# Linear attention's decay levels: prefix sums and exponentials replaced by running products of block decays, on 64x64 quarters of the array

## The chip, the cores and the metric

The kernel runs on one core of one Trainium2 chip. The metric is the device time of one execution in microseconds; lower is better. Three runs of the kernel before took 316.83, 316.96 and 317.05 us (median 316.96 us).

## The reference, cut to what matters

One decoder layer on 256 tokens of width 1024. One input projection of the normalised x feeds two kinds of heads side by side: eight softmax heads of 64 (here each query simply attends causally, since 256 tokens are one block) and four heads of gated linear attention with key width 64 and value width 128. Their outputs are joined, projected and added to x; a gated feed-forward part with a short causal convolution and a last normalisation follow.

The linear attention is the part that changes. With a decay alpha per token and key channel:

```
S_t = diag(alpha_t) S_{t-1} + k_t^T v_t ;  o_t = q_t S_t
A[t,s] = sum_d q[t,d] k[s,d] prod_{s < u <= t} alpha[u,d]     (s <= t)
o = A v
```

So every pair (t, s) needs the product of the decays between s and t, per channel.

## The kernel before, in words

**The whole.** Matmuls against weights are done in three passes (`mm3`, L108): each operand is split into a rounded high part and the rest, and high x high, high x low and low x high are added. ScalarE makes the high parts of the weights (L92), VectorE the low parts (L95). Small attention matmuls are plain fp32, which the array takes as two passes each. TensorE's instructions stand in the order in which the program writes them (`manual_schedule` for PE); the order on VectorE and ScalarE is laid out by the framework's scheduler from dependencies and priority, with the softmax steps raised (`tc.high_priority`).

**The order around the change.** Steps q = 0 to 47 run the input projection: six groups of eight steps (gate inputs, softmax q, softmax k, softmax v, linear v, linear gate r), each step one slice of 128 of the contraction, twelve `mm3` passes of 256 columns or six of 512. Steps 48 to 63 are the output projection, and after them comes the feed-forward part. A table `plan`, filled by `on(q, f, ...)` (L537), names what is written ahead of the matmuls of step q: at equal q, in the order in which it was entered. The attention work thus lies between projection matmuls.

**Linear attention.** The gate is a log-sigmoid (`g_gate`, L301); `g_scan` (L314) makes its running sum `Gc` within each 128 tokens. The 128x128 score blocks are made by levels b = 32, 16, 8, 4, 2, 1, 64: at level b, a query in the second half of a 2b-token block meets the keys in its first half, with the block's middle as pivot. `lvl_a` (L321) subtracts on VectorE (L330, L331) and exponentiates on ScalarE (L332); `lvl_b` (L335) multiplies keys (L345) and, for each of the two heads of a pair, queries (L351) into zero-padded buffers `kts` and `qts`; `lvl_c` (L353) does eight matmuls on 128x64 halves of the array (L363; level 64: four with 128 columns on one half, L358); `lvl_d_` (L368) copies the level's entries out of PSUM by a mask (L377). `l128_a` to `l128_c` (L383 to L405) do the same between the two 128-token halves. `g_av` (L413) multiplies by v at step 46. The levels' matmuls stand at steps 25, 27, 30, 33, 36, 38 and 41, those of `l128_c` at 44.

**Softmax heads.** `m_scores` (L480) makes the scores of two heads on 64x128 halves of the array (L487), at steps 30, 33, 36 and 39; `m_softmax1` and `m_softmax2` (L490, L504), `m_pt` (transposes, L515) and `m_av` (L527, L528; steps 38, 41, 44 and 47) follow.

**PSUM.** Four banks (`acc`) serve the projections; four (`att`) are handed out in turn to everything else: each level, each score tile, each transpose and each `m_av` takes the next one and waits until its last reader is done.

Of the kernel before, what the change touches and what calls it, by code (L numbers as in the profile page):

```python
# [22 lines left out]
TAU = 16.0  # L23
# [1 line left out]
NP = DFF // 128  # L25
EPS = 1e-6
NG = 256 + RANK + 256
LEVELS = [32, 16, 8, 4, 2, 1, 64]

P_FG, P_BG, P_CW, P_CB = 0, 8, 10, 10 + 3 * 2 * NP  # L30
NPAR = P_CB + 2 * NP
# [3 lines left out]
def trunk_kernel(ctx: ExitStack, tc: tile.TileContext, xT_d, wG_d, w5_d, wo_d, up_d, dn_d,  # L35
                 par_d, gla_g_d, fin_g_d, wgu_d, cos_d, sin_d, causal_d, lvl_d, ident_d, out_d):
    nc = tc.nc
    V, A, T, DMA = nc.vector, nc.scalar, nc.tensor, nc.sync
# [11 lines left out]
    def att():  # L50
        return ps_att.tile([128, 512], F32, name="att")
# [7 lines left out]
    lvl = const.tile([128, len(LEVELS), 32], F32, name="lvl")  # L59
# [140 lines left out]
    at = ap_.enter_context(tc.tile_pool(name="attn", bufs=1))  # L200
    gqk = at.tile([128, 2, NG], F32, name="gqk")
    gqT = at.tile([128, 2, S], F32, name="gqT")
    gkT = at.tile([128, 2, S], F32, name="gkT")
    Gc = at.tile([128, 512], F32, name="Gc")
    ATd = at.tile([128, 8, 64], F32, name="ATd")
    AT = at.tile([128, 8, 128], F32, name="ATf")
    AT01 = at.tile([128, 4, 128], F32, name="AT01")
    lrT = at.tile([RANK, S], F32, name="lrT")
    kts = [at.tile([128, 512], F32, name=f"kt{i}") for i in range(2)]
    qts = [at.tile([128, 4, 2, 64], F32, name=f"qt{i}") for i in range(2)]  # L210
    qt128 = at.tile([128, 2, 2, 128], F32, name="qt128")
    resets = at.tile([128, 512], F32, name="y", bufs=2)
    nc.gpsimd.memset(resets, 1.0)
    nc.gpsimd.memset(resets.rearrange("p (n t) -> p n t", t=128)[:, :, 0:1], 0.0)
    for i in range(2):
        nc.gpsimd.memset(kts[i], 0.0)
        nc.gpsimd.memset(qts[i], 0.0)
    nc.gpsimd.memset(qt128, 0.0)
    nc.gpsimd.memset(AT[64:128, :, 0:64], 0.0)
    mqT = at.tile([128, 4, S], F32, name="mqT")  # L220
    mkT = at.tile([128, 4, S], F32, name="mkT")
# [9 lines left out]
    st = {}  # L231
# [41 lines left out]
    def g_transpose(which):  # L273
        p = att()
        o, dst, sc = ((0, gqT, DK ** -0.5), (272, gkT, 1.0))[which]
        for pr in range(2):
            for tt in range(2):
                c = pr * S + tt * 128
                T.transpose(p[:, c:c + 128], gqk[:, tt, o + pr * 128:o + (pr + 1) * 128], ident)
        A.activation(dst.rearrange("p a t -> p (a t)"), p, AF.Copy, scale=sc)  # L280

    def g_diag():
        dgp = at.tile([128, 2, 256], F32, name="e", bufs=2)
# [27 lines left out]
        A.activation(e, e, AF.Ln, bias=1.0)  # L311
        st["mn"], st["ln"] = mn, e

    def g_scan():  # L314
        la = at.tile([128, 512], F32, name="d", bufs=2)
        V.tensor_sub(la, st["mn"], st["ln"])
        V.tensor_tensor_scan(Gc, resets, la, 0.0, op0=ALU.mult, op1=ALU.add)

    lv = {}

    def lvl_a(l):  # L321
        b = LEVELS[l]
        d = at.tile([128, 512], F32, name="d", bufs=2)
        e = at.tile([128, 512], F32, name="e", bufs=2)
        dv = d.rearrange("p (n two b) -> p n two b", two=2, b=b)
        gvw = Gc.rearrange("p (n two b) -> p n two b", two=2, b=b)
        n = 256 // b
        piv = gvw[:, :, 0, b - 1:b]
        pb = piv.to_broadcast([128, n, b])
        V.tensor_sub(dv[:, :, 0, :], pb, gvw[:, :, 0, :])  # L330
        V.tensor_sub(dv[:, :, 1, :], gvw[:, :, 1, :], pb)  # L331
        A.activation(e, d, AF.Exp, scale=1.0 / TAU)  # L332
        lv[l] = e

    def lvl_b(l):  # L335
        b = LEVELS[l]
        e = lv[l]
        kt, qt = kts[l % 2], qts[l % 2]

        def blk(x):  # L340
            return x.rearrange("p (n two b) -> p n two b", two=2, b=b)

        gk_ = gkT.rearrange("p a t -> p (a t)")
        gq_ = gqT.rearrange("p a t -> p (a t)")
        V.tensor_mul(blk(kt)[:, :, 0, :], blk(gk_)[:, :, 0, :], blk(e)[:, :, 0, :])  # L345
        for h in range(2):
            ps = slice(64 * h, 64 * h + 64)
            o = qt[ps, :, h, :].rearrange("p g (n b) -> p g n b", b=b)
            q_ = gq_[ps].rearrange("p (g n two b) -> p g n two b", g=4, two=2, b=b)[:, :, :, 1, :]
            e_ = e[ps].rearrange("p (g n two b) -> p g n two b", g=4, two=2, b=b)[:, :, :, 1, :]  # L350
            V.tensor_mul(o, q_, e_)  # L351

    def lvl_c(l):  # L353
        kt, qt = kts[l % 2], qts[l % 2]
        p = att()
        if LEVELS[l] == 64:
            for g in range(4):
                T.matmul(p[0:64, g * 128:(g + 1) * 128], kt[:, g * 128:g * 128 + 64],  # L358
                         qt[:, g].rearrange("p h t -> p (h t)"), start=True, stop=True)
        else:  # L360
            for g in range(4):
                for j in range(2):
                    T.matmul(p[64 * j:64 * j + 64, g * 64:(g + 1) * 64],  # L363
                             kt[:, g * 128 + 64 * j:g * 128 + 64 * j + 64],
                             qt[:, g, :, 32 * j:32 * j + 32], start=True, stop=True)
        st["lv", l] = p

    def lvl_d_(l):  # L368
        b = LEVELS[l]
        p = st["lv", l]  # L370
        if b == 64:
            A.activation(AT[0:64, :, 64:128], p[0:64].rearrange("p (i t) -> p i t", i=8), AF.Copy)
            return
        n = 32 // b
        o = ATd.rearrange("p i (n two b) -> p i n two b", two=2, b=b)[:, :, :, 1, :]
        m = lvl[:, l].bitcast(I32).rearrange("p (n b) -> p n b", b=b)[:, None].to_broadcast([128, 8, n, b])
        V.copy_predicated(o, m, p[:, :256].rearrange("p (i n b) -> p i n b", i=8, b=b))  # L377
# [5 lines left out]
    def l128_a():  # L383
        d = at.tile([128, 2, 128], F32, name="d", bufs=2)
        e = at.tile([128, 2, 2, 128], F32, name="e", bufs=2)
        G4 = Gc.rearrange("p (a b t) -> p a b t", a=2, b=2)
        V.tensor_sub(d, G4[:, :, 0, 127:128].to_broadcast([128, 2, 128]), G4[:, :, 0, :])
        A.activation(e[:, 0], d, AF.Exp, scale=1.0 / TAU)
        A.activation(e[:, 1], G4[:, :, 1, :], AF.Exp, scale=1.0 / TAU)
        lv["128"] = e  # L390

    def l128_b():
        e = lv["128"]
        kt = kts[1].rearrange("p (a t) -> p a t", a=4)
        V.tensor_mul(kt[:, 0:2], gkT[:, :, 0:128], e[:, 0])
        for h in range(2):
            ps = slice(64 * h, 64 * h + 64)
            V.tensor_mul(qt128[ps, :, h, :], gqT[ps, :, 128:256], e[ps, 1])

    def l128_c():  # L400
        p = att()
        for pr in range(2):
            T.matmul(p[:, pr * 256:(pr + 1) * 256], kts[1][:, pr * 128:(pr + 1) * 128],
                     qt128[:, pr].rearrange("p h t -> p (h t)"), start=True, stop=True)
        A.activation(AT01.rearrange("p a t -> p (a t)"), p, AF.Copy)  # L405

    def gv_evac(tt):
        A.activation(gv[:, tt], st["gv"][tt], AF.Copy, scale=rstd(tt))
# [70 lines left out]

    def m_scores(pr):  # L480

        for hh in range(2):
            st["s", 2 * pr + hh] = att()
        for c0, c1 in ((0, 128), (128, 384)):
            for hh in range(2):
                ps = slice(64 * hh, 64 * hh + 64)
                T.matmul(st["s", 2 * pr + hh][:, c0:c1], mqT[ps, pr, c0:c0 + 128], mkT[ps, pr, 0:c1 - c0],  # L487
                         start=True, stop=True)

    def m_softmax1(h):  # L490
        with tc.high_priority():
# [45 lines left out]
    def on(q, f, *a):  # L537
        plan.setdefault(q, []).append((f, a))
# [21 lines left out]
    on(16, g_diag)  # L560
    on(12, g_gate_mm)
    on(12, g_gate)
    on(14, g_scan)
    for l in range(7):
        b = 21 + 11 * l // 4
        on(b, lvl_a, l)
        on(b + 1, lvl_b, l)
        on(b + 4, lvl_c, l)
        on(b + 5, lvl_d_, l)
    on(b + 5, lvl_join)  # L570
    on(39, l128_a)
    on(42, l128_b)
    on(44, l128_c)
    for tt in range(2):
        on(19 + 3 * tt, rope_b, 0, tt)
        on(27 + tt, rope_b, 1, tt)
        on(32, mv_evac, tt)
        on(40, gv_evac, tt)
    for h in range(HM):
        b = 30 + 3 * h // 2  # L580
        if h % 2 == 0:
            on(b, m_scores, h // 2)
        on(b + 1, m_softmax1, h)
        on(b + 2, m_softmax2, h)
        on(b + 4, m_pt, h)
        if h % 2:
            on(b + 7, m_av, h // 2)
    on(46, g_av, 0)
    on(46, g_av, 1)
    on(49, g_tail)  # L590
# [22 lines left out]
    for q in range(48):  # L613
        g, k = divmod(q, 8)
# [34 lines left out]
    for q in range(48, 64):  # L649
        ph, j = divmod(q - 48, 8)  # L650
# [264 lines left out]
    n = NP - 1  # L915
# [115 lines left out]
```

## Time and profile before

| what | value |
|---|---|
| median of three runs | 316.96 us |
| the profiled execution | 317.14 us, its span 315.4 us |
| granted TensorE clock, mean | 0.996 |
| TensorE busy | 306.6 us (97% of the span), 2296 matmul passes |
| VectorE busy | 252.9 us (80%), 472 instructions |
| ScalarE busy | 203.8 us (65%), 370 instructions |
| GpSimd busy | 3.9 us (1%) |

The span is the time from the first to the last instruction of the profiled execution; 1.7 us of its time lie around it. TensorE matmuls are pipelined, so their ends overlap: how fast the array goes is read from the distance between starts, not from busy time.

### The profile page before, as it was taken

The numbers are of one execution on the slowest core, as the hardware profiler recorded it, in microseconds if no ns is written. First come the engines' busy times: TensorE is split into PE (matmuls) and PEld (weight loads), VectorE is DVE, ScalarE is ACT, GpSimd is POOL, SyncE is SP. The second block draws the span as 40 slices with busy tenths as digits, with TensorE's granted clock in tenths as the row PEclk, the third lists the DMA queues.
The fourth block names the chain that finished last, engine by engine and source line by source line (L and its number), as shares of the span: only waits on it lengthen the run. The fifth ranks groups of instructions, "written<-read, shape, count | busy, mean of one in ns | idle before, by whom it ended". The sixth has DMA issues, their size and how long they took to land.

```text
span 315.4 us, 5840 instructions
## 1 busy us (share of the span) xinstructions
PE 306.6 (97%) x2296; PEld 283.1 (90%) x2296; DVE 252.9 (80%) x472; ACT 203.8 (65%) x370; POOL 3.9 (1%) x17
## 2 busy tenths in 40 slices
PE   7899999999999999999999999999999999999992
PEld 6899997776888999999999999999999999999982
DVE  3887999999647677999999988877777777776643
ACT  5878989497858478367676556666665555544362
POOL 4000000000000000000000000000000000000000
PEclk9999999999999999999999999999999999999998
DMA  7999533342361525496555664545555622120003
GB/s 199 374 413 411 201 135 133 133 150 120 135 219 50 178 90 200 157 380 268 200 202 200 225 220 177 195 185 202 201 202 200 262 72 69 67 69 0 2 0 135
DMA packets 12444, 55.40 MB, mean 176 GB/s; under 512 B 1392, under 2 KB 3200, under 8 KB 8064
## 3 DMA queue, kind: packets, MB, share of 16 engines
q1 hardware_dynamic: 12272, 54.76, 47.2%
q8 instruction: 18, 0.29, 0.3%
q10 hardware_dynamic: 144, 0.26, 0.2%
q14 instruction: 10, 0.08, 0.1%
HBM read 53.97 MB, written 1.05 MB: 174 GB/s over the span
## 4 chain that ended last, share of the span: by engine, by line
PE 79%; DVE 9%; ACT 5%; issue 2%; DMA 2%; SPq 1%; DVEq 0%; ACTq 0%
PE att L109 14%; PE att L111 14%; PE att L110 14%; PE acc L110 11%; PE acc L109 10%; PE acc L111 10%; DVE lo L95 2%; DMA xg<-in_xT 2%; ACT qs L466 1%; DVE qt L351 1%; DVE att L495 1%; ACT hi L92 1%; PE att L527 1%; DVE ATd L377 1%; DVE kt L345 1%
## 5 line engine op out<-in xcount | busy, mean ns | idle before, releaser
L92 ACT ACTIVATE hi<-raw 128x1024 fp32r<-128x1024 f32 (+3 forms) x84 | 80.1, 971 | 50.9 <-PE att L110 43.2
L95 DVE TENSOR_TENSOR lo<-raw,hi 128x1024 fp32r<-128x1024 f32 (+3 forms) x86 | 93.7, 1098 | 13.3 <-ACT hi L92 13.2
L109 PE MATMUL att<-hh,hi 128*128 128x256 f32 x352 | 98.5, 280 | 0.0
L111 PE MATMUL att<-hh,lo 128*128 128x256 f32 x352 | 98.4, 279 | 0.0
L110 PE MATMUL att<-hl,hi 128*128 128x256 f32 x352 | 98.3, 279 | 0.0
L109 PEld LDWEIGHTS att<-hh,hi 128*128 128x128 f32 x352 | 66.2, 188 | 0.0
L111 PEld LDWEIGHTS att<-hh,lo 128*128 128x128 f32 x352 | 66.2, 188 | 0.0
L110 PEld LDWEIGHTS att<-hl,hi 128*128 128x128 f32 x352 | 66.2, 188 | 0.0
L757 DVE SCALAR_TENSOR_TENSOR c<-us,par,c 128x256 f32<-128x256 f32 x88 | 40.7, 482 | 4.1 <-ACT c L749 2.5
L749 ACT ACTIVATE c<-us,par 128x256 f32<-128x256 f32 x44 | 24.0, 591 | 21.5 <-DVE us L739 16.0
L111 PE MATMUL acc<-dhi,gl 128*128 128x512 f32 (+1 forms) x88 | 32.3, 367 | 0.0
L110 PE MATMUL acc<-dlo,gh 128*128 128x512 f32 (+1 forms) x88 | 32.2, 366 | 0.0
L109 PE MATMUL acc<-dhi,gh 128*128 128x512 f32 (+1 forms) x88 | 31.8, 361 | 0.0
L696 DVE TENSOR_TENSOR dlo<-draw,dhi 128x1024 fp32r<-128x1024 f32 x22 | 26.6, 1218 | 0.0
L739 DVE TENSOR_TENSOR us<-att,rb 128x512 f32<-128x512 f32 x20 | 13.8, 688 | 15.9 <-PE att L111 15.9
L109 PE MATMUL acc<-hi,ah 128*128 128x512 f32 (+1 forms) x64 | 25.6, 399 | 0.7 <-ACT hi L92 0.7
L110 PE MATMUL acc<-lo,ah 128*128 128x512 f32 (+1 forms) x64 | 24.2, 378 | 0.7 <-DVE lo L95 0.7
L111 PE MATMUL acc<-hi,al 128*128 128x512 f32 (+1 forms) x64 | 23.7, 371 | 0.0
L691 ACT ACTIVATE dhi<-draw 128x1024 fp32r<-128x1024 f32 x22 | 23.1, 1050 | 0.0
L110 PEld LDWEIGHTS acc<-dlo,gh 128*128 128x128 f32 x88 | 16.5, 188 | 3.0
L109 PEld LDWEIGHTS acc<-dhi,gh 128*128 128x128 f32 x88 | 16.6, 188 | 2.9
L111 PEld LDWEIGHTS acc<-dhi,gl 128*128 128x128 f32 x88 | 16.5, 188 | 2.6
(191 smaller groups left out, 528.9 us busy)
## 6 DMA issues: line engine op xcount, KB each, us to landing
raw<-in_up SPq DMA_DIRECT2D x22, 1024.0 KB, 4.8
draw<-in_dn SPq DMA_DIRECT2D x22, 512.0 KB, 5.7
raw<-in_w SPq DMA_DIRECT2D x8, 1024.0 KB, 7.3
raw<-in_wo SPq DMA_DIRECT2D x4, 1024.0 KB, 4.8
raw<-in_w SPq DMA_DIRECT2D x4, 512.0 KB, 8.1
raw<-in_wG SPq DMA_DIRECT2D x2, 528.0 KB, 7.3
raw<-in_wG SPq DMA_DIRECT2D x3, 264.0 KB, 4.0
xg<-in_xT SPq DMA_DIRECT2D x2, 256.0 KB, 6.4
```

The source lines that it names most:

```text
L92: A.activation(self.hi[:, a:b], self.raw[:, a:b], AF.Copy)
L95: V.tensor_sub(self.lo[:, a:b], self.raw[:, a:b], self.hi[:, a:b])
L109: T.matmul(out, sh, mh, start=first, stop=False, **kw)
L110: T.matmul(out, sh, ml, start=False, stop=False, **kw)
L111: T.matmul(out, sl, mh, start=False, stop=last, **kw)
L345: V.tensor_mul(blk(kt)[:, :, 0, :], blk(gk_)[:, :, 0, :], blk(e)[:, :, 0, :])
L351: V.tensor_mul(o, q_, e_)
L691: A.activation(hi, downs[i][0], AF.Copy)
L696: V.tensor_sub(lo, d, hi)
L739: V.tensor_tensor(u[:, :, 2:], upo[i][2].rearrange("p (a t) -> p a t", a=2), rb[:, None, :].to_broadcast([128, 2, S]), op=ALU.mult)
L749: A.activation(cv[i][:, a], u[:, a, 2:], AF.Identity, bias=par[:, P_CB + m:P_CB + m + 1], scale=par[:, P_CW + 2 * 2 * NP + m:P_CW + 2 * 2 ...
L757: V.scalar_tensor_tensor(c[:, a], u[:, a, w:w + S], par[:, wc:wc + 1], c[:, a], op0=ALU.mult, op1=ALU.add)
```

## The change

- Instead of running sums and exponentials of differences, the decay itself is exponentiated once (`g_decay`, `dec[0]`), and each next level's block decays are products of two neighbours (`dec[l]`).
- Keys and queries are multiplied **in place**, level after level from b = 1 up: at each level half of the queries and half of the keys take the neighbour block's decay (`lvl_u`, `lvl_u64`). The zero-padded buffers and their GpSimd memsets go. A second copy of the keys (`gk1`) and the odd queries (`q1`) keep what level 1 needs.
- The levels' matmuls run on **64x64 quarters**: per level 16 matmuls of 64 rows, 64 weights' columns and 32 moving columns, one head in each row half.
- Levels 1 and 2 go together at step 24 (`lvl_first`). Levels 4, 8, 16 and 32 go ahead of the scores of one pair of softmax heads each and are written into columns 384 to 511 of those two banks; the scores too are made on quarters. The level of 64 and the block between the two halves of 128 go together at step 44 (`lvl_last`), evicted by four ScalarE copies at step 45.
- The mask copies are now two per level, one per head of a pair.
- The last pair of softmax heads moves by one step: scores from step 39 to 40, its `m_av` from step 47 to 48, where the output projection starts.

The diff, cut to its core:

```diff
-LEVELS = [32, 16, 8, 4, 2, 1, 64]
+LEVELS = [1, 2, 4, 8, 16, 32]
...
         A.activation(dst.rearrange("p a t -> p (a t)"), p, AF.Copy, scale=sc)
+        if which:
+            A.activation(gk1.rearrange("p a t -> p (a t)"), p, AF.Copy)
...
-    def g_scan():
+    def g_decay():
         la = at.tile([128, 512], F32, name="d", bufs=2)
         V.tensor_sub(la, st["mn"], st["ln"])
-        V.tensor_tensor_scan(Gc, resets, la, 0.0, op0=ALU.mult, op1=ALU.add)
+        A.activation(dec[0], la, AF.Exp, scale=1.0 / TAU)
...
+    def lvl_u(l):
         b = LEVELS[l]
+        if l == 0:
+            V.tensor_mul(q1, two(gqf, 1)[:, :, 1, 0], two(dec[0], 1)[:, :, 1, 0])
+            V.tensor_mul(two(gqf, 1)[:, :, 0, 0], two(gqf, 1)[:, :, 0, 0], two(dec[0], 1)[:, :, 0, 0])
+            return
+        c = b // 2
+        dc = two(dec[l - 1], 1)
+        n = 512 // b
+        q = q1.rearrange("p (n c) -> p n c", c=1) if l == 1 else two(gqf, c)[:, :, 1]
+        V.tensor_mul(two(gqf, c)[:, :, 1], q, dc[:, :, 0].to_broadcast([128, n, c]))
+        V.tensor_mul(two(gkf, c)[:, :, 0], two(gkf, c)[:, :, 0], dc[:, :, 1].to_broadcast([128, n, c]))
+        V.tensor_mul(dec[l], dc[:, :, 0, 0], dc[:, :, 1, 0])
...
+    def lvl_c(l, p, c):
         b = LEVELS[l]
+        for g in range(4):
+            for j in range(2):
+                for h in range(2):
+                    ps = slice(64 * h, 64 * h + 64)
+                    a = g * 128 + 64 * j
+                    q = q1[ps, a // 2:a // 2 + 32] if l == 0 else two(gqf[ps, a:a + 64], b)[:, :, 1]
+                    k = gk1.rearrange("p a t -> p (a t)") if l == 0 else gkf
+                    T.matmul(p[h][64 * j:64 * j + 64, c + 32 * g:c + 32 * g + 32], k[ps, a:a + 64], q,
+                             start=True, stop=True)
...
+    def lvl_last():
+
+        p = [att() for _ in range(2)]
+        for g in range(4):
+            for h in range(2):
+                ps = slice(64 * h, 64 * h + 64)
+                T.matmul(p[h][0:64, g * 64:(g + 1) * 64], gkf[ps, g * 128:g * 128 + 64],
+                         gqf[ps, g * 128 + 64:(g + 1) * 128], start=True, stop=True)
+        for pr in range(2):
+            for t, q in enumerate((gqT[:, pr, 128:192], q128[:, pr])):
+                for j, k in enumerate((k128[:, pr], gkT[:, pr, 64:128])):
+                    for h in range(2):
+                        ps = slice(64 * h, 64 * h + 64)
+                        c = 256 + pr * 128 + 64 * t
+                        T.matmul(p[h][64 * j:64 * j + 64, c:c + 64], k[ps], q[ps], start=True, stop=True)
...
     def m_scores(pr):
 
+        p = [att() for _ in range(2)]
+        lvl_c(pr + 2, p, 384)
+        for c0, c1 in ((0, 128), (128, 384)):
+            for j in range(2):
+                for hh in range(2):
+                    ps = slice(64 * hh, 64 * hh + 64)
+                    a = c0 + 64 * j
+                    T.matmul(p[hh][64 * j:64 * j + 64, c0:c1], mqT[ps, pr, a:a + 64], mkT[ps, pr, 0:c1 - c0],
+                             start=True, stop=True)
...
-    on(14, g_scan)
-    for l in range(7):
-        b = 21 + 11 * l // 4
-        on(b, lvl_a, l)
-        on(b + 1, lvl_b, l)
-        on(b + 4, lvl_c, l)
-        on(b + 5, lvl_d_, l)
-    on(b + 5, lvl_join)
-    on(39, l128_a)
-    on(42, l128_b)
-    on(44, l128_c)
+    on(14, g_decay)
+    on(15, lvl_u, 0)
+    on(19, lvl_u, 1)
+    on(24, lvl_first)
+    on(25, lvl_d_, 0)
+    on(25, lvl_d_, 1)
+    on(26, lvl_u, 2)
...
-        b = 30 + 3 * h // 2
+        b = (30, 33, 36, 40)[h // 2] + h % 2
         if h % 2 == 0:
             on(b, m_scores, h // 2)
+            on(b + 1, lvl_d_, 2 + h // 2)
+            if h == 6:
+                on(b + 1, lvl_join)
+            on(b + 2, *((lvl_u, 3 + h // 2) if h < 6 else (lvl_u64,)))
...
+    on(44, lvl_last)
+    on(45, lvl_last_d)
```

## Rows read from the trace of the kernel before

**Rows 1.** Page, the chain of work that ended last, by engine.

```profile
PE 79%; DVE 9%; ACT 5%; issue 2%; DMA 2%; SPq 1%; DVEq 0%; ACTq 0%
```

**Rows 2.** 40 to 80 us: length; busy PE, PEld, DVE, ACT, POOL; clock.

```profile
40.00:80.00 40.00, 39.42 (x297) 30.62 (x297) 39.68 (x106) 31.84 (x69) 0.00 (x0) 1.00 0.38 134
```

**Rows 3.** TensorE's timeline, step 30 (start us, us, operation): level, then scores.

```profile
55.05 0.40 PE L111 MATMUL acc<-hi,al 128*128 128x512 f32 x1
55.38 0.69 PE L363 MATMUL att<-qt,kt 128*64 128x64 f32 x16
55.99 0.93 PE L487 MATMUL att<-mkT,mqT 64*128 64x128 f32 x8
...
57.18 0.40 PE L110 MATMUL acc<-lo,ah 128*128 128x512 f32 x1
...
60.91 0.40 PE L111 MATMUL acc<-hi,al 128*128 128x512 f32 x1
```

**Rows 4.** Timeline of TensorE, step 39: around scores without a level.

```profile
76.24 0.40 PE L111 MATMUL acc<-hi,al 128*128 128x512 f32 x1
...
77.76 0.40 PE L110 MATMUL acc<-lo,ah 128*128 128x512 f32 x1
```

**Rows 5.** Timeline of TensorE, step 25: around a level by itself.

```profile
46.42 0.40 PE L111 MATMUL acc<-hi,al 128*128 128x512 f32 x1
...
47.70 0.40 PE L110 MATMUL acc<-lo,ah 128*128 128x512 f32 x1
```

**Rows 6.** TensorE, step 38: level, `m_av`, transposes; [idle before <- releaser].

```profile
72.30 0.40 PE L111 MATMUL acc<-hi,al 128*128 128x512 f32 x1
...
73.89 0.66 PE L527 MATMUL att<-pt,mv 128*64 128x256 f32 x4 [0.58 <-ACT pe L500]
...
75.31 0.39 PE L110 MATMUL acc<-lo,ah 128*128 128x512 f32 x1
```

**Rows 7.** Timeline of TensorE, step 41: around level 64, `m_av`, transposes.

```profile
80.41 0.40 PE L111 MATMUL acc<-hi,al 128*128 128x512 f32 x1
...
83.08 0.39 PE L110 MATMUL acc<-lo,ah 128*128 128x512 f32 x1
```

**Rows 8.** Timeline of TensorE, step 44: `l128_c`, `m_av`, transposes.

```profile
87.14 0.40 PE L111 MATMUL acc<-hi,al 128*128 128x512 f32 x1
...
88.33 0.66 PE L527 MATMUL att<-pt,mv 128*64 128x256 f32 x4
...
89.75 0.39 PE L110 MATMUL acc<-lo,ah 128*128 128x512 f32 x1
```

**Rows 9.** TensorE: a level's first passes; passes behind 128-column loads.

```profile
55.38 0.28 PE L363 MATMUL att<-qt,kt 128*64 128x64 f32 x2
...
19.44 0.28 PE L248 MATMUL att<-ones,s 128*128 128x1 f32 x2
...
19.44 0.50 PE L248 MATMUL att<-ones,s 128*128 128x1 f32 x4
```

**Rows 10.** VectorE groups, 33 to 83 us: busy us, mean ns, idle.

```profile
L351 DVE TENSOR_TENSOR qt<-gqT,e 64x256 f32<-64x256 f32 x14 | 5.8, 415 | 0.1
...
L377 DVE COPY_PREDICATED ATd<-lvl,att 128x256 f32<-128x256 int32 x6 | 3.2, 536 | 0.1
...
L330 DVE TENSOR_TENSOR d<-Gc 128x256 f32<-128x256 f32 x7 | 2.9, 419 | 0.0
```

**Rows 11.** Timeline of VectorE: an instruction written at step 32.

```profile
60.63 0.42 DVE L330 TENSOR_TENSOR d<-Gc 128x256 f32<-128x256 f32 x1
```

**Rows 12.** Timeline of ScalarE: first squares after `g_av`; [idle before <- releaser].

```profile
93.40 0.28 ACT L430 ACTIVATE e<-att 128x128 f32<-128x128 f32 x1 [2.68 <-PE att L422]
```

**Rows 13.** Timelines: last `m_av` on TensorE (step 47); its low part on VectorE.

```profile
96.96 0.40 PE L528 MATMUL att<-pt,mv 128*64 128x128 f32 x4
...
97.83 0.42 DVE L532 TENSOR_TENSOR ml<-att,mh 128x256 fp32r<-128x256 f32 x1
```

More of the change, by code (lines that the diff above doesn't have):

```diff
@@ L203, in trunk_kernel @@
     gkT = at.tile([128, 2, S], F32, name="gkT")
-    Gc = at.tile([128, 512], F32, name="Gc")
+    gk1 = at.tile([128, 2, S], F32, name="gk1")
+    q1 = at.tile([128, 256], F32, name="q1")
+    dec = [at.tile([128, 512 >> i], F32, name=f"dec{i}") for i in range(7)]
+    q128 = at.tile([128, 2, 64], F32, name="q128")
+    k128 = at.tile([128, 2, 64], F32, name="k128")
     ATd = at.tile([128, 8, 64], F32, name="ATd")
@@ L208, in trunk_kernel @@
     lrT = at.tile([RANK, S], F32, name="lrT")
[L209 to L218, printed above, removed]
     nc.gpsimd.memset(AT[64:128, :, 0:64], 0.0)
@@ L312, in g_gate @@
         st["mn"], st["ln"] = mn, e
-    def g_scan():
+    def g_decay():
         la = at.tile([128, 512], F32, name="d", bufs=2)
         V.tensor_sub(la, st["mn"], st["ln"])
-        V.tensor_tensor_scan(Gc, resets, la, 0.0, op0=ALU.mult, op1=ALU.add)
-    lv = {}
-    def lvl_a(l):
-        b = LEVELS[l]
[L323 to L333, printed above, removed]
@@ L335, in lvl_b @@
-    def lvl_b(l):
-        b = LEVELS[l]
[L337 to L366, printed above, removed]
+        A.activation(dec[0], la, AF.Exp, scale=1.0 / TAU)
@@ new lines, in trunk_kernel, with two @@
+    gqf = gqT.rearrange("p a t -> p (a t)")
+    gkf = gkT.rearrange("p a t -> p (a t)")
+    def two(x, b):
+        return x.rearrange("p (n two b) -> p n two b", two=2, b=b)
+    def lvl_u(l):
+        b = LEVELS[l]
+        if l == 0:
[9 more added lines that the diff above has]
+        V.tensor_mul(dec[l], dc[:, :, 0, 0], dc[:, :, 1, 0])
@@ new lines, in lvl_u64 @@
+    def lvl_u64():
+        c = 32
+        dc = two(dec[5], 1)
+        V.tensor_mul(two(gqf, c)[:, :, 1], two(gqf, c)[:, :, 1], dc[:, :, 0].to_broadcast([128, 8, c]))
+        V.tensor_mul(two(gkf, c)[:, :, 0], two(gkf, c)[:, :, 0], dc[:, :, 1].to_broadcast([128, 8, c]))
+        V.tensor_mul(dec[6], dc[:, :, 0, 0], dc[:, :, 1, 0])
+        d6 = dec[6].rearrange("p (a b c) -> p a b c", a=2, b=2)
+        V.tensor_mul(q128, gqT[:, :, 192:256], d6[:, :, 1, 0:1].to_broadcast([128, 2, 64]))
+        V.tensor_mul(k128, gkT[:, :, 0:64], d6[:, :, 0, 1:2].to_broadcast([128, 2, 64]))
@@ new lines, in lvl_c @@
+    def lvl_c(l, p, c):
+        b = LEVELS[l]
+        for g in range(4):
[7 more added lines that the diff above has]
+                             start=True, stop=True)
+        st["lv", l] = (p, c)
@@ L368, in lvl_d_ @@
     def lvl_d_(l):
         b = LEVELS[l]
[L370 to L373, printed above, removed]
+        p, c = st["lv", l]
         n = 32 // b
-        o = ATd.rearrange("p i (n two b) -> p i n two b", two=2, b=b)[:, :, :, 1, :]
-        m = lvl[:, l].bitcast(I32).rearrange("p (n b) -> p n b", b=b)[:, None].to_broadcast([128, 8, n, b])
-        V.copy_predicated(o, m, p[:, :256].rearrange("p (i n b) -> p i n b", i=8, b=b))
+        for h in range(2):
+            o = ATd.rearrange("p (g h) (n two b) -> p g h n two b", h=2, two=2, b=b)[:, :, h, :, 1, :]
+            m = lvl[:, l].bitcast(I32).rearrange("p (n b) -> p n b", b=b)[:, None].to_broadcast([128, 4, n, b])
+            V.copy_predicated(o, m, p[h][:, c:c + 128].rearrange("p (g n b) -> p g n b", g=4, b=b))
@@ L379, in lvl_join, with lvl_first @@
+    def lvl_first():
+        p = [att() for _ in range(2)]
+        for l in range(2):
+            lvl_c(l, p, 128 * l)
     def lvl_join():
@@ L381, in lvl_join, with lvl_last_d @@
         A.activation(AT[0:64, :, 0:64], ATd[0:64], AF.Copy)
[L383 to L395, printed above, removed]
-        for h in range(2):
[L397 to L405, printed above, removed]
+    def lvl_last():
[8 more added lines that the diff above has]
+                for j, k in enumerate((k128[:, pr], gkT[:, pr, 64:128])):
+                    for h in range(2):
+                        ps = slice(64 * h, 64 * h + 64)
+                        c = 256 + pr * 128 + 64 * t
+                        T.matmul(p[h][64 * j:64 * j + 64, c:c + 64], k[ps], q[ps], start=True, stop=True)
+        st["last"] = p
+    def lvl_last_d():
+        for h in range(2):
+            p = st["last"][h]
+            A.activation(AT.rearrange("p (g h) t -> p g h t", h=2)[0:64, :, h, 64:128],
+                         p[0:64, 0:256].rearrange("p (g t) -> p g t", g=4), AF.Copy)
+            A.activation(AT01.rearrange("p (a h) t -> p a h t", h=2)[:, :, h],
+                         p[:, 256:512].rearrange("p (a t) -> p a t", a=2), AF.Copy)
     def gv_evac(tt):
@@ L480, in m_scores @@
     def m_scores(pr):
-        for hh in range(2):
[L483 to L488, printed above, removed]
+        p = [att() for _ in range(2)]
+        lvl_c(pr + 2, p, 384)
[6 more added lines that the diff above has]
+                             start=True, stop=True)
+        for hh in range(2):
+            st["s", 2 * pr + hh] = p[hh]
     def m_softmax1(h):
```

## The prediction

> **What bounds the kernel now.** I read the chain of waits first, to see which engine carries the end: 79% of it is TensorE, 9% VectorE [rows 1]. VectorE's part lies in the attention stretch, so the next view is the busy time there: from 40 to 80 us VectorE is busy 39.68 us of 40, ScalarE 31.84, and TensorE 39.42 [rows 2]. Two engines look full, and what counts is which one makes the other wait. The timeline of TensorE answers: in 16 steps it starts a pass of 512 columns every (60.91 - 57.18) / 16 = 0.233 us [rows 3], also while VectorE is full, and in these 40 us it is idle once, for 0.58 us in step 38, waiting for a softmax exponential [rows 6]. So TensorE's order bounds the stretch, VectorE's queue shows only in that one wait, and a saving counts where it shortens what stands between projection matmuls.
>
> I price such a block from the start of the last projection pass before it to the start of the second one behind it, less two steps (0.467):
> - a level by itself: 47.70 - 46.42 - 0.467 = 0.81 us [rows 5];
> - level and scores: 57.18 - 55.05 - 0.467 = 1.66 [rows 3]; scores alone: 1.05 [rows 4];
> - step 38 (level, av, transposes): 2.54 [rows 6]; step 41 (level 64 in their place): 2.20 [rows 7]; step 44 (l128): 2.14 [rows 8].
>
> In a level's 16 passes, two start together, one per half of the array: the first two take 0.28 us together, where all 16 take 0.69 [rows 3, 9]. So a round of two is (0.69 - 0.28) / 7 = 0.0586 us, eight rounds are 0.47, and 0.34 of the 0.81 are edges: the array changes its division going in and out, and a first weight load lies open. One edge is 55.38 - 55.05 - 0.233 = 0.10 [rows 3]. In step 44, l128 takes from 87.14 + 0.233 to 88.33, 0.96 us, of which one edge stays with av. So av and transposes with all their edges are 2.14 - 0.96 + 0.10 = 1.28.
>
> **The change part by part.** *TensorE.* No row shows quarters. Halves by columns (level) and by rows (scores) each run two abreast, so I take four abreast. A round has half the moving columns of before but the same 64 columns of weights. Behind loads of 128 columns even a pass of one column takes (0.50 - 0.28) / 2 = 0.11 us [rows 9], so loads set the pace, 64 of them about 0.055, and I keep 0.0586. Bounds: 0.029 (the moving columns alone) and 0.117 (two abreast only).
> - Levels 1 and 2 together: 0.34 + 16 x 0.0586 = 1.28, for 2 x 0.81: -0.34.
> - Four score blocks with a level each, one division of the array for both: 1.05 + 0.47 - 0.04 (shorter first load) = 1.48 each, 5.92, for 3 x 1.66 + 1.05 = 6.03: -0.11.
> - Step 38 loses its level: 2.54 - 1.28 = 1.26, of which about 0.51 is the level and 0.75 the wait (0.58 idle, the rest the pipeline refilling).
> - Step 41 loses level 64, eight passes one after another: 2.20 - 1.28 = -0.92.
> - Step 44: l128 goes (-0.86), `lvl_last` comes: 24 matmuls in 16 rounds, 0.94 + 0.34 = 1.28. +0.42.
>
> Work alone: -0.34 - 0.11 - 0.51 - 0.92 + 0.42 = -1.46 us.
>
> *The wait in step 38.* There av takes the PSUM bank of the fifth head's scores, whose exponential is late because VectorE is. The change takes banks for levels out of the ring: av now gets the second transposes' bank, long free, and the score bank falls to the transposes behind it. VectorE also loses work: 14 query multiplies (5.8 us), seven key multiplies and 14 subtractions of 0.42 each, six mask copies (3.2) [rows 10], besides the scan and l128's. It gets some 15 multiplies of 256 elements (0.42), a few short ones and 12 mask copies of half size (at least 0.27 each, by halving): about 11 us for about 20. I count the 0.75 as gone; if it stays, the gain ends at 1.46.
>
> *Costed at nothing.* ScalarE's seven exponentials make way for one, a second key copy and four evictions in step 45. The evictions (256 columns, one to two of the 0.28 us that a 128x128 square takes [rows 12]: 1.1 to 2.2 in all) have 12 projection passes, 2.8 us, before `g_av` reads them, and ScalarE sat idle 2.68 us just there [rows 12]. Without that cover they cost up to 2.2 us. `m_av` of the last pair moves to step 48, past six projection passes. Behind it are its high and low parts, on ScalarE and VectorE, done 97.83 + 0.42 - (96.96 + 0.40) = 0.89 us after its passes [rows 13]; the output projection first has nine passes of 256 columns (half of 0.233 each, 1.05) that don't read them. Cover is just enough; if ScalarE's gate activations slip ahead, I allow 0.5. The softmax steps of that pair move by one step into slack. No DMA issue moves; one table is 1/7 smaller. GpSimd's memsets were at the start, off the path.
>
> *Waits added.* In-place multiplies must wait until the last level's matmuls have read keys and queries, and the next scores' block, three steps (4.2 us) on, waits for them. Queued behind them on VectorE is only other work with slack. Nothing if VectorE is prompt; the price if not is a rival below.
>
> Sum: -1.46 - 0.75 = -2.2 us on the profiled execution's 317.14, which is 0.18 over the median: **314.9, said as 314.8 us** against runs of 316.96.
>
> **The rivals.**
> *A. Waits eat part.* The bank wait stays, or small new ones come at steps 36 to 48: for it, VectorE's and ScalarE's orders are laid out anew; against it, 9 us less on VectorE. Gain 0.7 to 1.5: 315.5 to 316.3.
> *B. The in-place chain is late.* An instruction written at step 32 ran at 60.63 [rows 11], and TensorE wanted step 33 at 60.91 + 0.24 [rows 3]. Three multiplies (1.1 us) put there would hold TensorE 0.6 us, at steps 33, 36 and 40 alike: 1.8 us, or with the old wait 2.5. Time 316.6 to 317.3, no change. It decides when VectorE is over 2 us behind what is written; without half its level work it should not be.
> *C. Slower: quarters run only two abreast.* Then the change doesn't do what it says. Place: every block on quarters. Each level takes 0.47 more (six: 2.8), `lvl_last`'s second half 0.47, and each scores block, whose 0.85 us from 55.99 to the next projection pass holds some 0.65 of passes, another 0.65 (2.6). +5.9: 320.7. It turns to a loss once the 64 rounds of levels alone take over 0.0586 + 2.2/64 = 0.093 us. For it: no row has four. Against it: both kinds of halves overlap fully, and rows and columns are independent.
> *D. Passes have a floor of their own.* A level's 16 passes in 0.47 are 0.029 us a pass, the closest that these rows sustain. If that is a floor, 32 passes take 0.94: +2.8 for six levels, +0.47 for `lvl_last`, nothing for scores (16 passes in 0.65): 318.1. Against it: two passes start within 0.01 us of each other [rows 9].
> The Trainium skill, "TensorE: Matmul & The Clock Gate" (section "Wait — 56ns, not 53.3ns?"), states a start-to-start floor of about 25 ns however few the columns; by that rule a level is 0.8 us and D comes out at 317.1 as an estimate, no gain. That the first two starts are 0.01 us apart speaks against that rule across parts of the array; no row shows it sustained.
>
> **How the numbers follow.** Forecast (four abreast, waits gone, 314.1 to 315.2): 0.62. A: 0.18. B: 0.06. C: 0.07. D: 0.07, split over no change and slower. A measurement here tells about 0.2%, 0.6 us, from no change. Faster, the forecast and A: 0.80. Same, B and a little of D: 0.08. Slower, C and the rest of D: 0.12. The range 314.1 to 317.3 holds the forecast, A and B, and leaves out C, most of D, and rounds at 0.029 (about 313).
>
> **What would show it.** The level's 32 passes in about 0.47 us and level plus scores in 1.48; a block of 0.94 plus edges at step 44; step 38 at 1.28 without idle time; VectorE well below full from 40 to 80 us; no idle TensorE at steps 33, 36, 40, 46 and 48. From step 49 on the trace should be the same, shifted. I'm wrong if a level's passes spread over 0.9 us (C, D; scores of 1.3 mean C), or if TensorE waits for a multiply on keys or queries (B).

## The result, and the profile after

The changed kernel takes 314.91 us (median of four runs, 314.68 to 315.19) against 316.89 us of the kernel before beside it (316.72 to 317.05): a ratio of 0.9938, 95% interval 0.9921 to 0.9955, 2.0 us less. The forecast was 314.8 us, within 314.1 to 317.3. The profiled execution took 315.09 us with a span of 313.1 us, 2.3 less than before.

The chain that ended last, by engine (page of the changed kernel):

```profile
PE 94%; DMA 2%; DVE 1%; SPq 1%; issue 1%; ACT 0%; DVEq 0%; ACTq 0%
```

TensorE went from 79% of the chain to 94%, VectorE from 9% to 1% [rows 1]. Then the same 40 us as in [rows 2] (busy PE, PEld, DVE, ACT, POOL; clock):

```profile
40.00:80.00 40.00, 40.00 (x438) 31.31 (x437) 34.48 (x95) 29.74 (x63) 0.10 (x1) 1.00 0.45 159
```

TensorE has no idle time left; VectorE fell from 39.68 to 34.48 us, ScalarE from 31.84 to 29.74. What TensorE does between projection matmuls stands in its timeline (start us, us, operation): `lvl_first` at step 24, level and scores at step 30, `m_av` and transposes at step 38, all of step 44, and step 48.

```profile
45.20 0.28 PE L111 MATMUL acc<-ah,lo 128*128 128x256 f32 x1
45.41 0.67 PE L359 MATMUL att<-q,gk 64*64 64x32 f32 x32
45.90 0.65 PE L359 MATMUL att<-gqT,gkT 64*64 64x32 f32 x32
...
46.81 0.40 PE L110 MATMUL acc<-lo,ah 128*128 128x512 f32 x1
...
54.74 0.40 PE L111 MATMUL acc<-hi,al 128*128 128x512 f32 x1
55.07 0.67 PE L359 MATMUL att<-gqT,gkT 64*64 64x32 f32 x32
55.56 0.86 PE L488 MATMUL att<-mkT,mqT 64*64 64x128 f32 x16
...
56.69 0.39 PE L110 MATMUL acc<-lo,ah 128*128 128x512 f32 x1
...
71.34 0.40 PE L111 MATMUL acc<-hi,al 128*128 128x512 f32 x1
71.67 0.66 PE L530 MATMUL att<-pt,mv 128*64 128x256 f32 x4
72.15 0.40 PE L531 MATMUL att<-pt,mv 128*64 128x128 f32 x4
72.48 0.55 PE L518 MATMUL att<-ident,pe 128*128 128x128 f32 x3
...
73.10 0.40 PE L110 MATMUL acc<-lo,ah 128*128 128x512 f32 x1
...
84.13 0.40 PE L111 MATMUL acc<-hi,al 128*128 128x512 f32 x1
...
85.74 0.62 PE L387 MATMUL att<-gqT,gkT 64*64 64x64 f32 x14
...
86.26 0.22 PE L395 MATMUL att<-gqT,k 64*64 64x64 f32 x1
...
86.55 0.22 PE L395 MATMUL att<-gqT,k 64*64 64x64 f32 x1
86.55 0.22 PE L395 MATMUL att<-q,gkT 64*64 64x64 f32 x1
86.56 0.22 PE L395 MATMUL att<-gqT,k 64*64 64x64 f32 x1
86.56 0.22 PE L395 MATMUL att<-q,gkT 64*64 64x64 f32 x1
86.61 0.22 PE L395 MATMUL att<-q,k 64*64 64x64 f32 x1
...
86.67 0.23 PE L395 MATMUL att<-q,k 64*64 64x64 f32 x2
...
87.16 0.40 PE L110 MATMUL acc<-lo,ah 128*128 128x512 f32 x1
...
97.61 0.28 PE L109 MATMUL acc<-mh,hi 128*128 128x256 f32 x1
97.77 0.39 PE L110 MATMUL acc<-ml,hi 128*128 128x256 f32 x1
97.99 0.28 PE L111 MATMUL acc<-mh,lo 128*128 128x256 f32 x1
```

**Quarters run four abreast**: at 86.55 us four passes start within 0.01 us, the next four 0.06 later, and 32 passes of a level take 0.49 us (45.41 to 45.90). The same way of pricing as in the prediction (from the last projection pass ahead to the second behind, less their two steps) gives, for step 30, 56.69 - 54.74 - 0.467 = 1.48 us. All blocks from 40 to 101 us, in us:

| block | before | predicted | after |
|---|---|---|---|
| levels 1 and 2 | 1.62 | 1.28 | 1.26 |
| scores of four pairs, three levels before, four after | 6.06 | 5.92 | 5.91 |
| step 38 | 2.54 | 1.26 to 1.28, no wait | 1.29, no wait |
| step 41 | 2.20 | 1.28 | 1.29 |
| step 44 | 2.15 | 2.56 | 2.56 |
| the five other transposes | 1.72 | the same | 1.63 |
| `g_av`, last `m_av` | 3.69 | the same | 3.69 |
| new wait in step 48 | 0 | 0, at most 0.5 | 0.14 |
| all | 19.98 | | 17.77 |

The new wait is in the last three rows of the timeline: from 97.61 to 97.99, two steps take 0.38 us instead of 0.24, where the output projection wants the low part of the last pair.

### The profile page after: what moved, and what is told of

Same layout as the page of the kernel before. It is cut to its first block, busy times and chain, and to the rows that moved or that the text cites. A ratio compares the mean times of both kernels' runs of the same rounds, so it can differ in the third digit from the quotient of the medians.

```text
span 313.1 us, 6132 instructions
## 1 busy us (share of the span) xinstructions
PE 304.4 (97%) x2460; PEld 281.5 (90%) x2460; DVE 244.9 (78%) x460; ACT 200.5 (64%) x365; POOL 1.3 (0%) x10
## 4 chain that ended last, share of the span: by engine, by line
PE 94%; DMA 2%; DVE 1%; SPq 1%; issue 1%; ACT 0%; DVEq 0%; ACTq 0%
PE acc L109 15%; PE acc L110 15%; PE acc L111 14%; PE att L110 14%; PE att L111 14%; PE att L109 14%; DMA raw<-in_wG 2%; PE att L359 1%; PE att L518 1%; PE att L488 1%; PE att L530 1%; PE att L421 1%; PE acc L796 0%; DVE lo L95 0%; SPq L154 0%
```

## The experiments

Ratios are against the kernel before. Block prices come from one profile each. Outside the blocks a profile moves too: in the changed kernel and the runs built on it, the block of step 24 begins at 44.6 to 45.2 us, and what moves it lies in the first 14 us of each trace. So the blocks tell where the time went, and the medians hold their sum to about half a microsecond.

### What a pass costs TensorE

**Scores on halves again**, as in the kernel before:

```diff
-            for j in range(2):
-                for hh in range(2):
...
-                    T.matmul(p[hh][64 * j:64 * j + 64, c0:c1], mqT[ps, pr, a:a + 64], ...
+            for hh in range(2):
+                T.matmul(p[hh][:, c0:c1], mqT[ps, pr, c0:c0 + 128], ...
```

> Theory (TensorE's written order bounds; each change of the array's division costs an edge): the level's quarters and the scores' halves now need a second change inside each score block, 0.1 us plus a first weight load of 128 columns lying open, 0.05 to 0.1. Each of the four score blocks goes from 1.48 to about 1.68 us: +0.8 us, about 315.7. Rival (the gain came from a lighter VectorE, TensorE's blocks have slack): no change, 314.9.

Measured: 315.15 us, ratio 0.9945 [0.9928, 0.9962]. Each of the four score blocks takes 1.65 instead of 1.48 us, and the sum of blocks is 0.71 more, as the theory had it. The median shows 0.24 of that and misses the expected 315.7; by medians alone this run can't be told from the changed kernel. Of the 0.17, 0.11 lies between level and scores, where the array changes its division (the scores begin 55.59 - 54.99 = 0.60 us behind the level instead of 0.49), the rest in and behind the scores.

**Each later level's passes twice:**

```diff
-        lvl_c(pr + 2, p, 384)
+        for _ in range(2):
+            lvl_c(pr + 2, p, 384)
```

> The four levels in the score blocks are written twice, to the same place. Theory (TensorE's order bounds, a level in a block that is on quarters anyway costs its eight rounds, 0.47 us): each score block goes from 1.48 to 1.95 us, +1.9 us, about 316.8. Rival (level matmuls lie in time that TensorE had to wait anyway): less than 0.6 us more.

Measured: 317.02 us, ratio 1.0005 [0.9995, 1.0014]. In its TensorE timeline, step 30, 64 passes take 0.96 us (54.72 to 55.68):

```profile
54.72 1.14 PE L359 MATMUL att<-gqT,gkT 64*64 64x32 f32 x64
55.68 0.86 PE L489 MATMUL att<-mkT,mqT 64*64 64x128 f32 x16
```

A level more costs 0.46 us (score blocks 1.94), as 8 x 0.0586 said. Step 36 has 2.57, with a wait of 0.34 for a softmax exponential on top: the cover there is not thick.

**One head's passes after the other's** (four quarters, other order of writing):

```diff
-        for g in range(4):
-            for j in range(2):
-                for h in range(2):
+        for h in range(2):
+            for g in range(4):
+                for j in range(2):
```

> All 16 passes of one head's rows are written before the other head's. If the array takes passes in the order written, only two quarters run at a time: 16 rounds of 0.058 instead of 8 for each of six levels, +0.47 each, +2.8 us, about 317.7. If it lets passes for idle quarters go past waiting ones over a distance of 16 passes, nothing changes: 314.9, with a level still taking about 0.47 us. In between if it looks ahead less far.

Measured: 315.98 us, ratio 0.9971 [0.9961, 0.9982]; score blocks 1.73 (0.25 more), `lvl_first` 1.58 (0.32 more). The second head's quarters start at 55.17, 0.27 us after the first head's at 54.90, right behind the latter's tenth pass of 16. So the array overlaps only what stands a few passes apart in the order written. Within that reach starts don't keep to the order: the first score pass, written behind the level, starts ahead of the level's last six.

```profile
55.43 0.32 PE L488 MATMUL att<-mkT,mqT 64*64 64x128 f32 x1
55.48 0.28 PE L359 MATMUL att<-gqT,gkT 64*64 64x32 f32 x3
```

**One quarter after another:**

```diff
-        for g in range(4):
+        for h in range(2):
             for j in range(2):
-                for h in range(2):
+                for g in range(4):
```

> The changed kernel with each level's passes written one quarter after another (the four steps in depth innermost) instead of all four quarters of one depth side by side. Theory (TensorE starts a pass of another quarter only if it is written a few passes ahead, about six as the run with the heads apart showed): a level takes about 17 rounds of 58 ns, 1.0 us instead of .47, so score blocks of about 2.0 instead of 1.48 and the first level longer by .5 or more: about 317.5 us. Rival (any quarter that is free starts, whatever the order): no change, 314.9 us. If the passes ran strictly in the order written with no overlap, 32 rounds: 1.9 us a level, and over 321 us.

Measured: 319.19 us, ratio 1.0072 [1.0057, 1.0087]: slower than before the change. Score blocks take 2.24 us, `lvl_first` 2.60. Single starts of L359 in step 30 (us), the first five of the first quarter and the first of the others:

```
first quarter   56.203 56.282 56.340 56.398 56.457
second quarter  56.463
third quarter   56.723
fourth quarter  56.983
```

Each quarter begins right behind the fifth of eight passes of the one written ahead of it, 0.26 us later; 3 x 0.26 = 0.78 is what the block grew by (0.76). The run before fits the same rule: its tenth pass of 16 is the fifth pass of the second of two quarters. A matmul is two passes, so five passes reach into the third matmul. The reading is that instructions are taken in order (though not started in it), and each quarter holds one matmul beside the one that it works on. A reach of a fixed number of passes over the whole array doesn't fit: three passes were still to start here, six in the run before. The depth itself is inferred from these two runs and no other run tests it. I had expected 17 rounds a level and 317.5 us; about 21 came (8 + 0.78 / 0.058), because I had counted six passes ahead where three are.

### Where the wait of step 38 went

**One PSUM bank more handed out at step 38** of the changed kernel, with two passes of its own:

```diff
+    def more_bank():
+        p = att()
+        T.matmul(p[:, :128], warm, warm, start=True, stop=True)
+        V.tensor_copy(sm[:, 32:64], p[:, 0:32])
...
+            on(38, more_bank)
```

> The changed kernel with one more bank taken ahead of av in step 38: two passes of 128 columns into it (0.22 us) and a VectorE copy that reads it. Theory (a bank too few is what makes av wait there): av or the transposes behind it wait again for a score bank, whose exponential ended at 73.1 us where av started at 71.7: step 38 gets idle time of 0.5 to 1.2 us, 315.6 to 316.3. Rival (the wait went with VectorE's load): only the passes' 0.25 us, about 315.1.

Measured: 315.19 us, ratio 0.9951 [0.9932, 0.9969]; step 38 takes 1.99 instead of 1.29 us, of which the two passes are 0.22 and the wait, with the refilling behind it, 0.48. TensorE's waits from 40 to 103 us (for what: us in total, times, longest):

```profile
PE att L518 <- ACT pe L503: 0.4, 1, 0.4
```

The transposes of step 38 wait again for the fifth head's exponential. The wait is thus one bank away, and the exponential is still late. (The median alone, 0.28 us up, would fit the rival's 315.1; it is the trace that decides.) ScalarE's timeline shows it, first of the kernel before, then of the changed one:

```profile
72.92 0.37 ACT L500 ACTIVATE pe<-att,mx 128x128 f32<-128x128 f32 x1 [1.66 <-DVE mx L497]
```

```profile
72.22 0.37 ACT L503 ACTIVATE pe<-att,mx 128x128 f32<-128x128 f32 x1 [1.36 <-DVE mx L500]
```

It starts 0.70 us earlier than before, but TensorE reaches `m_av` 73.31 - 71.67 = 1.64 earlier, 0.5 of it the level that left this block. In both kernels ScalarE had waited over 1.3 us for the maxima from VectorE.

**Free columns alone**: the kernel before, with its levels 8, 4, 2 and 1 written into the score banks' free columns. The level of 1 moves with that from step 38 to 39, and VectorE gets four mask copies more.

```diff
+SHARED = (2, 3, 4, 5)
...
+        lvl_c(SHARED[pr], [st["s", 2 * pr + hh] for hh in range(2)])
...
-        on(b + 4, lvl_c, l)
-        on(b + 5, lvl_d_, l)
+        if l not in SHARED:
+            on(b + 4, lvl_c, l)
+            on(b + 5, lvl_d_, l)
```

> One part of the change alone: the kernel before, with its exponentials and its 128x64 halves, but four of its levels (8, 4, 2, 1) go into columns 384 to 511 of the score banks, and the level of 1 moves from step 38 to the last score block. VectorE gets four mask copies more. Theory (a bank too few): no idle time in step 38, -0.75 us; the moved level costs 0.61 in its new block for 0.51 in its old one: about 316.3. Rival (VectorE's lateness): the wait stays, 316.9 to 317.1.

Measured: 316.90 us, ratio 1.0003 [0.9993, 1.0012]. Step 38 takes 1.29 us without a wait: `m_av` starts at 72.97, though the fifth head's exponential starts only at 73.58, later than in the kernel before (72.92), and VectorE is as full as before (third busy time of the row, 40 to 80 us):

```profile
40.00:80.00 40.00, 39.79 (x298) 30.99 (x298) 39.69 (x110) 30.74 (x67) 0.00 (x0) 1.00 0.38 136
```

But the expected 316.3 us didn't come. The moved level costs 0.62 at step 39, and step 36 takes 2.10 instead of 1.67 us. TensorE's timeline of this kernel shows a new wait there, in the middle of the level:

```profile
68.41 0.45 PE L360 MATMUL att<-qt,kt 128*64 128x64 f32 x8 [0.21 <-ACT pt L534]
```

So the banks alone end the wait of step 38, and put a smaller one ahead of a score block.

**Fewer subtractions alone**: the kernel before without the 14 subtractions on VectorE (each level exponentiates the running sum itself; the differences are left out).

```diff
-        V.tensor_sub(dv[:, :, 0, :], pb, gvw[:, :, 0, :])
-        V.tensor_sub(dv[:, :, 1, :], gvw[:, :, 1, :], pb)
-        A.activation(e, d, AF.Exp, scale=1.0 / TAU)
+        A.activation(e, Gc, AF.Exp, scale=1.0 / TAU)
```

> The kernel before without its 14 level subtractions (the exponential is taken of the running sum itself, so the levels' values are others): 4.7 us less on VectorE, the same banks and the same TensorE work. Theory (a bank too few in step 38): the wait of 0.75 us in step 38 stays, about 316.9. Rival (VectorE's lateness makes it): the wait is gone, about 316.2.

Measured: 317.19 us, ratio 1.0011 [1.0000, 1.0022]. With 5.8 us less on VectorE the wait of step 38 stays; the list of TensorE's waits from 40 to 103 us has this one line:

```profile
PE att L525 <- ACT pe L498: 0.5, 1, 0.5
```

Steps 36 and 39 grew by 0.51 and 0.26. The run has a limit: the fifth head's exponential starts at 73.27, 0.35 us later than before, behind scores that end 0.42 later, so less work on VectorE brought it hardly nearer to its scores. What would happen with maxima that are early isn't shown.

**Both together:**

```diff
+SHARED = (2, 3, 4, 5)
...
-        V.tensor_sub(dv[:, :, 0, :], pb, gvw[:, :, 0, :])
-        V.tensor_sub(dv[:, :, 1, :], gvw[:, :, 1, :], pb)
```

> The kernel before with both of the changes that did nothing one by one: the levels of 8, 4, 2 and 1 write into the score banks' free columns, and the 14 subtractions on VectorE are left out (the levels' values are therefore others). Theory (a bank must come free and VectorE must be lighter, both together): steps 36 and 38 run without waits, 1.67 and 1.29 us instead of 2.10 and 1.29 in the run with the free columns alone; the moved level adds its .61 to step 39; about 1.25 - .61 = .64 us under the kernel before, 316.2 us. Rival (ScalarE's exponentials alone hold the banks): a wait of about .4 us remains at step 36 or beside it, 316.7 us.

Measured: 317.53 us, ratio 1.0018 [1.0009, 1.0027]. Step 38 has no wait, step 36 takes 1.88 us, but step 39 takes 2.77. The list of TensorE's waits again:

```profile
PE att L358 <- DVE ml L547: 0.9, 1, 0.9
```

Here the level's second half waits for the bank of step 38's `m_av`, whose low part VectorE made only at 75.81 us. Both the theory and the rival fall: lighter VectorE beside free banks is not enough in the old kernel, whose order the scheduler lays out anew each time.

**The changed kernel with levels by running sums and exponentials** (quarters, places and order kept, no products in place):

```diff
-    on(14, g_decay)
-    on(15, lvl_u, 0)
-    on(19, lvl_u, 1)
+    on(14, g_scan)
+    for l, x in enumerate((24, 24, 30, 33, 36, 40, 44)):
+        on(x - 4, lvl_a, l)
+        on(x - 3, lvl_b, l)
```

> The changed kernel's quarters, order and places in PSUM, but the decays of the levels formed as in the kernel before, by running sums and exponentials, with no products in place. Theory (TensorE's shorter blocks and the banks make the gain, the running products themselves don't): score blocks 1.48, step 38 1.29, step 44 2.56 us, no waits, 314.9 to 315.3 us. Rival (the lighter VectorE and ScalarE of the products are needed as well): waits of .5 us or more in all at steps 33 to 40, 315.5 us or more.

Measured: 315.52 us, ratio 0.9958 [0.9945, 0.9971]. The blocks are those of the changed kernel but for step 36, 2.05 us. The list of TensorE's waits:

```profile
PE att L361 <- ACT pe L505: 0.3, 1, 0.3
```

So the products in place are worth 315.52 - 314.91 = 0.6 us, the rest of the gain does without them: the rival is right, at the low end. (The intervals overlap; the block of step 36 grew by as much, 0.57.) Exponentials of levels stand ahead of the softmax exponential that was waited for, on ScalarE:

```profile
66.19 0.62 ACT L332 ACTIVATE e<-d 128x512 f32<-128x512 f32 x1
66.71 0.35 ACT L505 ACTIVATE pe<-att,mx 128x128 f32<-128x128 f32 x1
```

I took them for the cause, but VectorE's timeline says otherwise. Here is the instruction that ends the maxima which that exponential needs, with the low part of a weight ahead of it, and then the same instruction in the changed kernel:

```profile
64.18 1.23 DVE L95 TENSOR_TENSOR lo<-raw,hi 128x1024 fp32r<-128x1024 f32 x1 [0.16 <-ACT hi L92]
...
66.32 0.16 DVE L502 TENSOR_SCALAR mx<-mx 128x2 f32<-128x2 f32 x1
```

```profile
64.75 0.16 DVE L500 TENSOR_SCALAR mx<-mx 128x2 f32<-128x2 f32 x1
```

The maxima were 66.32 - 64.75 = 1.57 us late, and the level's exponential held ScalarE only 66.71 - (66.32 + 0.16) = 0.23 us beyond them. In the changed kernel a low part runs behind these maxima, at 64.82. So it is the order on VectorE that made step 36 wait here.

The last two runs add ScalarE's and VectorE's part one by one. **Seven exponentials more** on ScalarE at those steps, nobody reading them:

```diff
+    def more():
+        A.activation(busy, st["la"], AF.Exp, scale=1.0 / TAU)
...
+    for x in (24, 24, 30, 33, 36, 40, 44):
+        on(x - 4, more)
```

> The changed kernel with seven exponentials of 512 columns more on ScalarE, at the steps at which the run with the levels by exponentials has them (nobody reads their result); VectorE is left as it is. Theory (the .61 us that the levels by exponentials cost came from ScalarE, where two exponentials of .62 us ran ahead of the softmax exponential that step 36 waited for): step 36 takes about 2.05 instead of 1.48 us, 315.4 us. Rival (it came from VectorE, or takes both): step 36 stays at 1.48, 314.9 us.

Measured: 315.59 us, ratio 0.9964 [0.9950, 0.9978]. The median is as the theory said, the place is not, and with it the theory falls: step 36 takes 1.48 us, and steps 34 and 40 wait, for the last softmax step on ScalarE (0.54 and 0.16 us idle; their blocks grew by 1.14 in all). They stand together in the list of TensorE's waits:

```profile
PE att L524 <- ACT pe L516: 0.7, 2, 0.5
```

These transposes wait for their data, not for a bank. And ScalarE was not too busy there: it had been idle for 2.14 us ahead of the softmax exponentials of step 34. What made them late lies 17 us back, where three of the added exponentials stand ahead of the copies and the high parts of weights on ScalarE. Rows of ScalarE, VectorE and ScalarE of this run:

```profile
43.84 1.94 ACT L325 ACTIVATE busy<-d 128x512 f32<-128x512 f32 x3
...
51.74 1.23 DVE L95 TENSOR_TENSOR lo<-raw,hi 128x1024 fp32r<-128x1024 f32 x1 [0.39 <-ACT hi L92]
...
61.18 0.37 ACT L509 ACTIVATE pe<-att,mx 128x128 f32<-128x128 f32 x1 [2.14 <-DVE mx L506]
```

The last two in the changed kernel:

```profile
50.79 1.22 DVE L95 TENSOR_TENSOR lo<-raw,hi 128x1024 fp32r<-128x1024 f32 x1 [0.40 <-ACT hi L92]
...
60.23 0.37 ACT L503 ACTIVATE pe<-att,mx 128x128 f32<-128x128 f32 x1 [0.80 <-DVE mx L500]
```

VectorE waits for a high part, starts its low part 0.95 us later, and carries the same 0.95 through its full queue to the maxima and so to the exponentials.

**Fourteen VectorE operations more** at the same steps:

```diff
+    def more():
+        for i in range(2):
+            V.tensor_mul(busy[:, 256 * i:256 * i + 256], st["la"][:, 0:256], st["la"][:, 256:512])
```

> The changed kernel with 14 operations of 256 elements more on VectorE, two at each of the steps at which the run with the levels by exponentials has its subtractions (nobody reads their result); ScalarE is left as it is. Theory (ScalarE's exponentials alone made the .61 us): no wait, step 36 at 1.48 us, 314.9 us. Rival (VectorE's load made it): a wait of .5 us or so at step 36, 315.4 us; if both are needed together, neither this run nor the one with the exponentials shows it.

Measured: 315.04 us, ratio 0.9948 [0.9933, 0.9963], which the changed kernel's interval takes in. Its trace has no wait of TensorE from 40 to 103 us, and step 36 takes 1.48, though VectorE is busy 37.22 us of the 40:

```profile
40.00:80.00 40.00, 40.00 (x437) 31.20 (x436) 37.22 (x105) 29.34 (x63) 0.10 (x1) 1.00 0.44 159
```

So VectorE operations of this number and size alone cost nothing that can be told, and the exponentials alone cost 0.68. That this is about the 0.61 of all the old decay work is partly chance: the waits lie at other steps. How the 0.61 divides between the engines stays open.

VectorE is not free without bound, though. **Fifteen multiplies of 512 elements more** (0.68 us each, 10.1 in all), three behind each level's products:

```diff
+    def more():
+        for _ in range(3):
+            V.tensor_mul(busy, gqf, gkf)
...
+        if l > 1:
+            more()
```

> 15 multiplies of 512 columns into a tile that nobody reads are added behind the in-place ones from level 4 on, some 9 us of VectorE, about what the change took away. Theory (the wait of step 38 went because banks for levels left the pool): VectorE is full again from 40 to 80 us, step 38 still has no idle time, and the time stays within 0.3 us of 314.9. Rival (it went because VectorE is lighter): a wait of 0.5 us or more comes back in step 38 or at the score blocks, 315.5 or more.

Measured: 316.87 us, ratio 1.0002 [0.9992, 1.0013], the whole gain gone; the theory, which allowed 0.3 us, missed by 2.0. The list of TensorE's waits from 40 to 103 us:

```profile
PE att L368 <- ACT pt L529: 0.7, 1, 0.7
PE att L527 <- DVE pe L520: 0.6, 1, 0.6
PE att L368 <- DVE gkT L341: 0.3, 1, 0.3
```

They lie at steps 36, 40 and 33, all of them steps with scores, as the rival had it; step 38 still has none, as the theory had it. The last row is the prediction's rival B: the scores' block waits for a product on the keys in place. It needs some 10 us more on VectorE than the change has; 5 us more (the run above) don't bring it.

## Why the prediction was right

The bound was read rightly: TensorE's written order sets the time, and each block that the change touches came out as priced, within 0.03 us. The sum of blocks fell by 2.21 where 2.2 was forecast; in it, 0.09 less on transposes and 0.14 of new wait, neither in the sum, about cancel.

- **Four abreast** (forecast 0.0586 us a round): held. A round is 0.49 / 8 = 0.061 with 32 moving columns and, in step 44, (86.67 - 86.26) / 7 = 0.059 with 64. Twice the columns in the same time agrees with loads setting the pace; no run changed the loads themselves. Rivals C and D are out. Four starts every 0.06 us are 15 ns a pass, below the 29 that D took for a floor. The Trainium skill, "TensorE: Matmul & The Clock Gate" (section "Wait — 56ns, not 53.3ns?"), with its 25 ns from start to start doesn't hold across quarters here; within one quarter, passes are 58 ns apart and don't touch it.
- **The wait of step 38** (0.75): gone, as counted, but only half of the reason stands. I gave two: the banks, and less work on VectorE. The run with the free columns alone ends that wait with VectorE full; the run without subtractions keeps it; one bank more brings 0.48 us of wait back. So it was the banks. I also had it that banks are handed out strictly in turn, and the transposes would take the score bank whose exponential is late. They ran at 72.48, while that exponential read its bank until 72.94 + 0.20 = 73.14, so they had another.
- **ScalarE's seven exponentials**, which I costed at nothing, are the term that I mis-sized. Put back by themselves they cost 0.68 us; of the 0.61 in the run that keeps all of the old decay work, their part is open. They cost this not by keeping ScalarE full but by making high parts of weights late, which VectorE passes on to the maxima. The sum came out right because I put the lack of new waits to VectorE's lighter queue alone, where the wait for ScalarE's high parts counts too.
- **VectorE's relief**: forecast some 9 us, measured 252.9 - 244.9 = 8.0. The 12 mask copies of half size take 3.3 us, no less than the six before (3.2).
- **Costed at nothing, and right**: the four evictions of step 45 took 0.36 to 0.38 us each from 87.18 on, well ahead of `g_av`'s block from 89.83. Behind the key copy `gk1` (0.57 us on ScalarE, at 26.75) TensorE has no wait up to 103 us.
- **Step 48** (cover just enough, 0.5 allowed): the output projection waited 0.14 us, but not by the way that I feared. A gate activation did run ahead of the high part, which still started 96.57 - (96.12 + 0.40) = 0.05 us behind its passes. The low part, wanted from 96.57 + 0.39 on, stood behind a gate multiply on VectorE, which I had not counted:

```profile
96.57 0.39 ACT L534 ACTIVATE mh<-att 128x256 fp32r<-128x256 f32 x1
...
96.69 0.69 DVE L450 TENSOR_TENSOR y<-y,gr 128x512 f32<-128x512 f32 x1 [0.28 <-ACT gr L410]
97.30 0.42 DVE L535 TENSOR_TENSOR ml<-att,mh 128x256 fp32r<-128x256 f32 x1
```

- **Rival A** (new waits of 0.7 to 1.5) was not seen. Its mechanism is real: three runs on the old kernel and four on the new one show such waits, at steps 33, 34, 36, 39 or 40.

## What to carry to other kernels

Between matmuls that can't be shortened, price each block from the row ahead of it to the second row behind it; changes of the array's division and rounds of passes then add up to the measured time within a few hundredths of a microsecond. Write small matmuls for parts of the array side by side, not one part after another: the same passes cost 319.19 - 314.91 = 4.3 us for their order alone, twice what the whole change gained. And where a wait names an exponential, ask first how many banks stand between it and the engine that waits: lightening an engine moved such waits about, one bank ended this one. Where no bank is short, follow the wait back past the engine that it names: that engine may have been idle itself, as ScalarE was.

## What the runs showed that I had not expected

- The order in which quarters are written decides whether they overlap. A further quarter starts only behind the fifth of the eight passes of the one ahead, 0.26 us late each time, and the kernel goes from 314.91 to 319.19 us.
- The less busy engine was the dearer one: 4.4 us of exponentials on ScalarE, idle for a quarter of the time, cost 0.68, while 5.2 us on VectorE, busier, cost nothing that can be told (0.13). What counted was what stood behind the added work: three exponentials at 43.84 us made a transpose wait at 63.8.
